# Diagonal of the row factors in the output ring, four loads of x together, and block sums' transfers on GpSimd

## The chip, the cores and the metric

The kernel runs on one core of one Trainium2 chip. The metric is the device time of one execution in microseconds. The time before is the median of three executions; a profile of one execution stands beside it.

## What is computed

The reference is one encoder layer on two token sequences, x_prompt (1024 tokens) and x_sample (2048 tokens) of 1024 channels, each with 16 learned meta tokens put in front. Cut to what matters:

```python
xn = rmsnorm(h, g_pre)
proj = xn @ w_in + b_in                 # 6672 columns: q, k, v, z of both branches, gates
ya = neighbourhood_attention(q, k, v, rpb) * silu(na_z) @ w_a
yb = mlstm_branch(qk, v, gates, o) * silu(ml_z) @ w_b       # both directions, chunks
y  = (sigmoid(ga) * ya + sigmoid(gb) * yb) @ w_out
out = h + rmsnorm(y, g_post)            # meta tokens dropped
```

All of it is float32. A product is made of three matmuls on a high and a low part of each operand (high x high, high x low, low x high), so every operand is first split: the high part is a ScalarE copy to the rounded type fp32r, the low part a VectorE subtraction.

## The kernel before

The program is written as two generators. `dense` makes the large products: the input projection in groups (`PLAN`: a sequence s, a block t0 of 1024 tokens, and a set of columns), then the output stage. `sparse` makes the mLSTM scan and the attention. `run` interleaves the two by estimated cost, and that fixes the order of TensorE's instructions. The order on the other engines (VectorE, ScalarE, GpSimd, and SP, which issues nearly all transfers) is set when the program is built, by a scheduler that simulates times. Each engine then runs its own queue in order.

**x.** A block of 512 tokens is held transposed in a pair of tiles xh and xl. `build_half` makes the pair beside the last products of the block before. For x_sample it loads four token tiles (`tokens`, SP, L398), sums their squares (`rsum`, ScalarE, L355), takes the reciprocal root on VectorE (`rsqrt8`), and writes the four row factors onto the diagonals of a 128 x 512 tile (`rdiag`, two operations on VectorE at L369 and two on ScalarE at L367). TensorE multiplies this by a matrix of ones (`rrows`, L375), which spreads the factors over all partitions, and ScalarE copies them out (L376). The transposed x comes in four loads of 512 KB (`xtload`, SP, L405); VectorE multiplies each with the factors (L527, two for each load), then each is split (L534 and L535). Token tiles and x loads share one ring, xr, of four tiles. The diagonal is written into the last token tile, so the fourth x load waits until the matmul has read it.

**The ring st.** `fm_evac` takes results of the projection out of PSUM into tiles named st, a ring of four in the pool wp, from which SP stores them (L698, L689). Columns with a SiLU, NZ and MZ, take two of these tiles (L678, L679, L680), the others one. A tile of a ring is given out again in the order of the program: the fifth takes the place of the first, once the first has been read.

**Block sums.** Where two halves of 512 tokens use the same weights, blocks of two by two are multiplied with seven products in place of eight (`sgates`, `_sw_order`). That needs sums of weight blocks and of x blocks. They are made as side work, a step every few products (`beside`):

- `wprep` does it for the gate columns: two loads of raw weights into pr (L579), four pairs of results in the one tile po (ScalarE L592, VectorE in `sub` at L571), eight stores (L596).
- `nprep` does it for the attention columns in the ring xr: two loads (L608), results split by ScalarE (L619) and VectorE (in `op` at L604), eight stores (L623, L624).
- `tprep` does it for x, four steps e for each of two blocks: eight stores a step (L653) into DRAM tensors t0h, t0l to t3h, t3l, which `tload` reads back later.

GpSimd (POOL) has little to do: memsets of a border column of the convolution's input raw (L1394, L1396), of the sums ss (L349) and of the scan's first state st (L1539, a tile of its own pool), some small copies, and the loads of the attention's constants (L1077, L1164).

Of the kernel before, what the change touches and what calls it, by code (L numbers as in the profile page):

```python
# [10 lines left out]
F32 = mybir.dt.float32  # L11
# [7 lines left out]
P = 128  # L19
TCARGS = dict(schedule_with_timeline_sim=True)  # L20
D = 1024
# [14 lines left out]
HALF = 528  # L36
# [17 lines left out]
PAIRS = [tuple(c[2 * p:2 * p + 2]) for c in (N_COLS, FM_COLS[24:]) for p in range(len(c) // 2)]  # L54
# [3 lines left out]
def _weight_units():  # L58

    return ([("i", x, P) for x in FM_COLS] + [("t", *c, a) for c in TM_COLS for a in range(2)]  # L60
            + [("m", f, P) for f in range(KT)] + [("o", c, a) for c in range(4) for a in range(2)])
# [76 lines left out]
class K:  # L138
# [327 lines left out]
    def build_half(self, s, t0, res):  # L466

        nc, wp = self.nc, self.wp
        if (s, t0) in self.xkept:
            assert not self.xput  # L470
            yield
            yield "scaled"
            x = []
            for name, part in zip(("xh", "xl"), self.xkept[s, t0]):
                x.append(wp.tile([P, KT, HALF], F32R, name=name, bufs=2))
                for k in range(0, KT, 4):
                    nc.sync.dma_start(x[-1][:, k:k + 4, :512].bitcast(F32), part[:, k:k + 4, :])
                yield
            res.append(tuple(x))
            return  # L480
        if s == 0:
            xts = self.xnext
            self.xnext = None
            while self.rwait:
                yield "wait"
            self.early = False
            yield "scaled"
            g = self.gpre
            p = self.psum("sm", [P, 512])
            nc.tensor.matmul(p[:, :KT], self.ident, g, start=True, stop=True)  # L490
            g = self.cp.tile([P, KT], F32, name="gx")
            nc.vector.tensor_copy(g, p[:, :KT])
            x, r = self.xparts(), []
            for e in range(4):
                self.xsplit(x, xts[e], e, 0, g)
                self.wflush(2)
                yield
            res.append(tuple(x))
            self.xkeep(s, 0, self.xs[0], NM)
            self.xkeep(s, t0, x)  # L500
            yield from self.rsum(self.toks, r)
            nc.vector.tensor_copy(self.rc[:, 4:8], r[0])
            dg = self.rdiag(r[0], self.toks[0][0])

            def rows():
                self.rrows(dg, self.rr[:, 1], "sm")
                self.RD = self.dp.tile([P, D], F32, name="rrd")
                nc.sync.dma_start(self.RD[:, :], self.rr.rearrange("p a t -> p (a t)"))
                self.xp.close()
                self.wside = self.wprep()  # L510
                self.sides.append([self.wside, 3])
            self.rwait[s, t0] = rows
        else:
            bp = self.bp
            toks, r = self.tokens(s, t0, range(4), bp, 4), []
            yield
            yield from self.rsum(toks, r)
            dg = self.rdiag(r[0], toks[3][0])
            xts = [self.xtload(s, t0, e, bp, 4) for e in range(3)]
            yield  # L520
            rr = bp.tile([P, 512], F32, name="rx", tag="thT", bufs=1)
            self.rrows(dg, rr, "pj")
            xts.append(self.xtload(s, t0, 3, bp, 4))
            yield
            for k in range(KT):
                v = xts[k // 2][:, k % 2]
                nc.vector.scalar_tensor_tensor(v, v, self.gpre[:, k:k + 1], rr, op0=ALU.mult, op1=ALU.mult)  # L527
                if k % 2:
                    yield
            yield "scaled"  # L530
            x = self.xparts()
            for e in range(4):
                h = x[0][:, 2 * e:2 * e + 2, :512]
                nc.scalar.activation(h, xts[e], AF.Copy)  # L534
                nc.vector.tensor_tensor(x[1][:, 2 * e:2 * e + 2, :512], xts[e], h.bitcast(F32), op=ALU.subtract)  # L535
                yield
            res.append(tuple(x))
            self.xkeep(s, t0, x)
# [28 lines left out]
    def wprep(self):  # L567

        nc = self.nc
        unit = {k: j for j, k in enumerate(_weight_units())}  # L570
        sub = lambda o, a, b: nc.vector.tensor_tensor(o, a, b, op=ALU.subtract)  # L571
        self.pq = ExitStack()
        pool = self.pq.enter_context(self.tc.tile_pool(name="pq", bufs=1, side="right", reuse_waits="tile"))
        for p in range(6, 14):
            if p == 12:
                self.sides[0][1] = 6
            raw = pool.tile([P, 2, 2, 512], F32, name="pr", bufs=1)
            for f in range(2):
                nc.sync.dma_start(raw[:, f].rearrange("p a c -> p (a c)"), self.i["wu"][unit["i", PAIRS[p][f], P], :, :D])  # L579
            for _ in range(3):  # L580
                yield
            for f, ops in ((0, ("11", "12")), (1, ("21", "22")), (1, ("s3", "s1")), (0, ("s2", "s4"))):
                if ops[0] == "s3":
                    nc.vector.tensor_tensor(raw[:, 1, 1], raw[:, 1, 0], raw[:, 1, 1], op=ALU.add)
                    sub(raw[:, 1, 0], raw[:, 0, 0], raw[:, 1, 0])
                    yield
                if ops[0] == "s2":
                    sub(raw[:, 0, 0], raw[:, 1, 1], raw[:, 0, 0])
                    sub(raw[:, 0, 1], raw[:, 0, 1], raw[:, 0, 0])
                    yield  # L590
                o = pool.tile([P, 2, 2, 512], F32R, name="po", bufs=1)
                nc.scalar.activation(o[:, :, 0], raw[:, f], AF.Copy)  # L592
                sub(o[:, :, 1], raw[:, f], o[:, :, 0].bitcast(F32))
                for q, op in enumerate(ops):
                    d = self.qd[p, op] = self.dp.tile([P, D], F32, name=f"q{p}{op}")
                    nc.sync.dma_start(d[:, :], o[:, q].rearrange("p a c -> p (a c)").bitcast(F32))  # L596
                yield
                yield

    def nprep(self):  # L600

        nc = self.nc
        unit = {k: j for j, k in enumerate(_weight_units())}
        op = lambda o, a, b, x=ALU.subtract: nc.vector.tensor_tensor(o, a, b, op=x)  # L604
        for p in range(6):
            r0, r1 = [self.bp.tile([P, 2, 512], F32, name="xr", bufs=4) for _ in range(2)]
            for f, r in enumerate((r0, r1)):
                nc.sync.dma_start(r.rearrange("p a c -> p (a c)"), self.i["wu"][unit["i", PAIRS[p][f], P], :, :D])  # L608
            for _ in range(2):
                yield  # L610
            op(r1[:, 1], r1[:, 0], r1[:, 1], ALU.add)
            op(r1[:, 0], r0[:, 0], r1[:, 0])
            yield
            op(r0[:, 0], r1[:, 1], r0[:, 0])
            op(r0[:, 1], r0[:, 1], r0[:, 0])
            yield
            for r, ops in ((r1, ("s3", "s1")), (r0, ("s2", "s4"))):
                hi = self.bp.tile([P, 2, 512], F32, name="xr", bufs=4)
                nc.scalar.activation(hi.bitcast(F32R), r, AF.Copy)  # L619
                op(r.bitcast(F32R), r, hi)  # L620
                for q, o in enumerate(ops):
                    d = self.qd[p, o] = self.dp.tile([P, D], F32, name=f"q{p}{o}")
                    nc.sync.dma_start(d[:, :512], hi[:, q])  # L623
                    nc.sync.dma_start(d[:, 512:], r[:, q])  # L624
                yield

    def tprep(self, s, t0):

        nc, dp = self.nc, self.dp
        self.TD[s, t0] = [[dp.tile([P, 4, 512], F32, name=f"t{j}{part}{t0}") for part in "hl"] for j in range(4)]  # L630
        td = self.TD[s, t0]
        while len(self.xs) < 2:
            yield
        (h0, l0), (h1, l1) = self.xs
        for e in range(4):
            ks = slice(2 * e, 2 * e + 2)
            r0, r1, ta, hi = [self.bp.tile([P, 2, 512], F32, name="xr", bufs=4) for _ in range(4)]
# [10 lines left out]
            for a, b, js in todo:  # L648
                nc.scalar.activation(a.bitcast(F32R), b, AF.Copy)
                nc.vector.tensor_tensor(b.bitcast(F32R), b, a, op=ALU.subtract)  # L650
                for q, j in enumerate(js):
                    for d, x in zip(td[j], (a, b)):
                        nc.sync.dma_start(d[:, e, :], x[:, q] if len(js) > 1 else x)  # L653
                yield


# [1479 lines left out]
```

## Time and profile before

| what | value |
|---|---|
| time, median of 3 | 2702.35 us (2702.05 to 2705.8) |
| profiled execution | 2705.33 us; its span, first to last instruction, 2703.3 us |
| mean granted TensorE clock | 0.995 |
| busy: TensorE, weight loads | 2658.4 us (98%), 2345.6 us (87%) |
| busy: VectorE, ScalarE, GpSimd | 1910.4 us (71%), 1418.5 us (52%), 17.4 us (1%) |
| transfers | 783.72 MB, mean 290 GB/s |

The profile's engines are PE (matmul) and PEld (weight load) for TensorE, DVE for VectorE, ACT for ScalarE, POOL for GpSimd, and SPq for SP's queue. A name such as L369 is a line of the kernel; work in a helper has the helper's line. In a row of the timeline the bracket holds the engine's idle time before the instruction and what ended it. The share of the granted clock is of full speed.

### The profile page before, as it was taken

How to read it: one execution, taken by the hardware profiler on the slowest of the kernel's cores; microseconds unless marked ns; L12 is line 12 of the kernel's file. 1: busy time of each engine (PE TensorE's matmuls, PEld its weight loads, DVE VectorE, ACT ScalarE, POOL GpSimd, SP SyncE). 2: the span in 40 equal slices, each digit the busy share in tenths (PEclk: the TensorE clock that was granted, in tenths of full speed). 3: DMA queues.
4: the chain of work that ended last, by engine and by line, in shares of the span. 5: the costliest groups of instructions: out<-in, count | busy, mean ns of one | idle time of the engine just before them, and what ended most of it. 6: DMA issues, size and time to landing. Idle time of an engine off the chain costs nothing.

```text
span 2703.3 us, 47407 instructions
## 1 busy us (share of the span) xinstructions
PE 2658.4 (98%) x16000; PEld 2345.6 (87%) x16000; DVE 1910.4 (71%) x5234; ACT 1418.5 (52%) x3350; POOL 17.4 (1%) x100
## 2 busy tenths in 40 slices
PE   9999998999999999999999999999999999999998
PEld 7898897789987999878888888888889888989888
DVE  5444687978648888446866767658478989897954
ACT  6322555565345654356655566555355655656521
POOL 0000000000000000000000000000000000000000
PEclk9999998999999999999999999999999999999999
DMA  9988887899986898798889988895769798998965
GB/s 373 344 323 316 306 302 277 295 348 345 317 270 228 295 349 298 248 305 259 262 288 329 368 288 258 282 344 189 219 221 303 250 312 257 309 294 262 333 230 202
DMA packets 405986, 783.72 MB, mean 290 GB/s; under 512 B 51472, under 2 KB 180448, under 8 KB 404208
## 3 DMA queue, kind: packets, MB, share of 16 engines
q1 hardware_dynamic: 404624, 778.01, 85.6%
q0 software_dynamic: 1120, 2.69, 0.4%
q8 instruction: 127, 2.08, 0.3%
q14 instruction: 115, 0.94, 0.1%
HBM read 531.66 MB, written 248.88 MB: 289 GB/s over the span
## 4 chain that ended last, share of the span: by engine, by line
PE 70%; DVE 6%; DMA 5%; ACT 2%; issue 1%; SPq 0%; DVEq 0%; ACTq 0%
PE pj L202 8%; PE pj L203 8%; PE pj L204 8%; PE pj L955 6%; PE pj L957 6%; PE pj L956 6%; PE pj L1898 3%; PE pj L1899 3%; PE pj L1900 3%; PE pj L762 3%; PE pj L763 3%; PE pj L764 3%; PE sm L1247 2%; PE tr L1232 2%; DMA stk<-nq 1%
## 5 line engine op out<-in xcount | busy, mean ns | idle before, releaser
L202 PE MATMUL pj<-xh,whi 128*128 128x512 f32 (+1 forms) x992 | 385.5, 389 | 2.7 <-ACT st L679 1.5
L203 PE MATMUL pj<-xl,whi 128*128 128x512 f32 (+1 forms) x992 | 375.3, 378 | 0.1
L204 PE MATMUL pj<-xh,wlo 128*128 128x512 f32 (+1 forms) x992 | 374.7, 378 | 0.2 <-DVE wlo L304 0.2
L762 PE MATMUL pj<-whi,xh 128*128 128x256 f32 (+1 forms) x1152 | 329.7, 286 | 0.0
L763 PE MATMUL pj<-wlo,xh 128*128 128x256 f32 (+1 forms) x1152 | 325.0, 282 | 0.6 <-DMA wlo<-wl 0.6
L764 PE MATMUL pj<-whi,xl 128*128 128x256 f32 (+1 forms) x1152 | 324.7, 282 | 0.0
L204 PEld LDWEIGHTS pj<-xh,wlo 128*128 128x128 f32 x992 | 188.0, 189 | 37.3 <-DVE wlo L304 0.4
L1898 PE MATMUL pj<-whi,mh 128*128 128x256 f32 x768 | 219.6, 286 | 0.7 <-DMA whi<-wh 0.7
L763 PEld LDWEIGHTS pj<-wlo,xh 128*128 128x128 f32 x1152 | 217.0, 188 | 1.0 <-DMA wlo<-wl 0.8
L202 PEld LDWEIGHTS pj<-xh,whi 128*128 128x128 f32 x992 | 188.2, 190 | 33.8 <-ACT st L679 2.0
L762 PEld LDWEIGHTS pj<-whi,xh 128*128 128x128 f32 x1152 | 217.1, 188 | 0.2
L764 PEld LDWEIGHTS pj<-whi,xl 128*128 128x128 f32 x1152 | 217.0, 188 | 0.0
L1900 PE MATMUL pj<-whi,mlo 128*128 128x256 f32 x768 | 216.4, 282 | 0.0
L1899 PE MATMUL pj<-wlo,mh 128*128 128x256 f32 x768 | 216.3, 282 | 0.0
L203 PEld LDWEIGHTS pj<-xl,whi 128*128 128x128 f32 x992 | 188.4, 190 | 28.9 <-issue 1.0
L202 PE MATMUL pj<-yh,whi 128*128 128x512 f32 x384 | 154.1, 401 | 0.0
L203 PE MATMUL pj<-yl,whi 128*128 128x512 f32 x384 | 150.8, 393 | 0.8 <-DVE yl L1800 0.8
L204 PE MATMUL pj<-yh,wlo 128*128 128x512 f32 x384 | 151.2, 394 | 0.0
L1898 PEld LDWEIGHTS pj<-whi,mh 128*128 128x128 f32 x768 | 145.2, 189 | 1.8 <-DMA whi<-wh 0.9
L1899 PEld LDWEIGHTS pj<-wlo,mh 128*128 128x128 f32 x768 | 145.4, 189 | 0.9
L1900 PEld LDWEIGHTS pj<-whi,mlo 128*128 128x128 f32 x768 | 145.3, 189 | 0.0
L1239 DVE TENSOR_TENSOR pts<-tr,pts 96x384 fp32r<-96x384 f32 (+2 forms) x192 | 118.7, 618 | 32.8 <-ACT pts L1234 31.1
(368 smaller groups left out, 6739.2 us busy)
## 6 DMA issues: line engine op xcount, KB each, us to landing
whi<-wh SPq DMA_DIRECT2D x136, 512.0 KB
wlo<-wl SPq DMA_DIRECT2D x136, 512.0 KB
whi<-q SPq DMA_DIRECT2D x63, 512.0 KB
wlo<-q SPq DMA_DIRECT2D x55, 512.0 KB
wraw<-wu SPq DMA_DIRECT2D x48, 512.0 KB
gt<-st SPq DMA_DIRECT2D x96, 256.0 KB
tg<-gt SPq DMA_DIRECT2D x96, 256.0 KB
wh<-whi SPq DMA_DIRECT2D x36, 512.0 KB
```

The lines of the kernel that those rows point to most:

```text
L202: mm(out, ah, bh, start=start, stop=False)
L203: mm(out, ah, bl, start=False, stop=False)
L204: mm(out, al, bh, start=False, stop=stop)
L762: nc.tensor.matmul(o, xh, wh, start=k == 0, stop=False)
L763: nc.tensor.matmul(o, xh, wl, start=False, stop=False)
L764: nc.tensor.matmul(o, xl, wh, start=False, stop=k == KT - 1)
L955: mm(bank, w[:, 0, k], xh[:, k], start=fresh and k == 0, stop=False, skip_group_check=True)
L956: mm(bank, w[:, 0, k], xl[:, k], start=False, stop=False, skip_group_check=True)
L957: mm(bank, w[:, 1, k], xh[:, k], start=False, stop=k == 3, skip_group_check=True)
L1898: nc.tensor.matmul(o, mh[:, k, xs], wh, start=clear > 0 and k == 0, stop=False)
L1899: nc.tensor.matmul(o, mh[:, k, xs], wl, start=False, stop=False)
L1900: nc.tensor.matmul(o, ml[:, k, xs], wh, start=False, stop=clear < 2 and k == KT - 1)
```

## The change

There are three parts.

- The diagonal of the row factors is written into a tile of the ring st and no more into the last token tile. All four x loads are then issued in one step; the fourth was issued a step later, after the matmul.
- The loads and stores of `wprep`, `nprep` and `tprep` are issued by GpSimd in place of SP.
- In `tprep` the x sums 0 and 1 lie in one DRAM tensor for the high parts and one for the low parts, and one transfer of 512 KB stores both sums of a part; before it was one transfer of 256 KB for each. `self.TD` hands out slices of them, so the loads that read them back are as before.

```diff
-            dg = self.rdiag(r[0], toks[3][0])
-            xts = [self.xtload(s, t0, e, bp, 4) for e in range(3)]
+            dg = self.rdiag(r[0], wp.tile([P, HALF], F32, name="st", bufs=4))
+            xts = [self.xtload(s, t0, e, bp, 4) for e in range(4)]
             yield
             rr = bp.tile([P, 512], F32, name="rx", tag="thT", bufs=1)
             self.rrows(dg, rr, "pj")
-            xts.append(self.xtload(s, t0, 3, bp, 4))
             yield
...
             for f in range(2):
-                nc.sync.dma_start(raw[:, f].rearrange("p a c -> p (a c)"), self.i["wu"][unit["i", PAIRS[p][f], P], :, :D])
+                nc.gpsimd.dma_start(raw[:, f].rearrange("p a c -> p (a c)"), self.i["wu"][unit["i", PAIRS[p][f], P], :, :D])
...
-                    nc.sync.dma_start(d[:, :], o[:, q].rearrange("p a c -> p (a c)").bitcast(F32))
+                    nc.gpsimd.dma_start(d[:, :], o[:, q].rearrange("p a c -> p (a c)").bitcast(F32))
...
             for f, r in enumerate((r0, r1)):
-                nc.sync.dma_start(r.rearrange("p a c -> p (a c)"), self.i["wu"][unit["i", PAIRS[p][f], P], :, :D])
+                nc.gpsimd.dma_start(r.rearrange("p a c -> p (a c)"), self.i["wu"][unit["i", PAIRS[p][f], P], :, :D])
...
-                    nc.sync.dma_start(d[:, :512], hi[:, q])
-                    nc.sync.dma_start(d[:, 512:], r[:, q])
+                    nc.gpsimd.dma_start(d[:, :512], hi[:, q])
+                    nc.gpsimd.dma_start(d[:, 512:], r[:, q])
...
-        self.TD[s, t0] = [[dp.tile([P, 4, 512], F32, name=f"t{j}{part}{t0}") for part in "hl"] for j in range(4)]
-        td = self.TD[s, t0]
+        t01 = [dp.tile([P, 2, 4, 512], F32, name=f"t01{part}{t0}") for part in "hl"]
+        td = {j: [dp.tile([P, 4, 512], F32, name=f"t{j}{part}{t0}") for part in "hl"] for j in (2, 3)}
+        self.TD[s, t0] = [[t[:, 0] for t in t01], [t[:, 1] for t in t01], td[2], td[3]]
...
-                for q, j in enumerate(js):
-                    for d, x in zip(td[j], (a, b)):
-                        nc.sync.dma_start(d[:, e, :], x[:, q] if len(js) > 1 else x)
+                for q, x in enumerate((a, b)):
+                    nc.gpsimd.dma_start(t01[q][:, :, e, :] if len(js) > 1 else td[js[0]][q][:, e, :], x)
```

## The prediction

> **What bounds the kernel now.** I read the page first, then the stretches of 60 us, then TensorE's timeline at the places where it stood still, and from there the queues that it waited for.
>
> ```profile
> PE 2658.4 (98%) x16000; PEld 2345.6 (87%) x16000; DVE 1910.4 (71%) x5234; ACT 1418.5 (52%) x3350; POOL 17.4 (1%) x100
> ...
> q1 hardware_dynamic: 404624, 778.01, 85.6%
> q0 software_dynamic: 1120, 2.69, 0.4%
> ...
> PE 70%; DVE 6%; DMA 5%; ACT 2%; issue 1%; SPq 0%; DVEq 0%; ACTq 0%
> ```
>
> TensorE is busy for 2658.4 of 2703.3 us, so all its idle time is 44.9 us, and its order is fixed by the program. The change takes no matmul away. It can win only idle time, and the time in which the clock is halved. GpSimd is nearly empty and its queue of transfers carries 0.4%.
>
> ```profile
> 420.00:480.00 60.00, 51.75 (x217) 41.64 (x216) 46.05 (x108) 36.85 (x82) 0.51 (x4) 0.89 0.80 286
> 480.00:540.00 60.00, 55.60 (x262) 45.79 (x262) 54.09 (x159) 34.78 (x83) 0.10 (x1) 0.94 0.81 286
> 540.00:600.00 60.00, 59.38 (x328) 50.84 (x327) 46.70 (x113) 38.17 (x93) 0.41 (x3) 1.00 1.00 353
> ...
> 780.00:840.00 60.00, 56.88 (x281) 46.30 (x280) 44.48 (x109) 37.61 (x76) 0.00 (x0) 1.00 0.65 219
> ```
>
> The columns are the stretch, its length, and busy time of PE, PEld, DVE, ACT, POOL, then granted clock, DMA share and GB/s. Two stretches stand out: 420 to 540 us loses 12.7 us of TensorE and runs below full clock. That is where the first two halves of x_sample are built. 780 to 840 loses 3.1. Inside the first there are three gaps:
>
> ```profile
> 432.12 0.47 PE L202 MATMUL sm<-vwh,kth 16*128 16x130 f32 x1 [3.00 <-ACT kth L1522]
> ...
> 460.09 0.55 PE L1648 MATMUL sc<-q,kh 128*128 128x256 f32 x1 [4.31 <-DVE nwy L166]
> ...
> 509.06 0.45 PE L202 MATMUL sm<-v,sh 128*128 128x130 f32 x1 [4.40 <-DVE num L1688]
> ...
> 2225.37 0.41 PE L1200 MATMUL sm<-kd,stk 128*128 128x384 f32 x1 [2.12 <-DVE yg L1262]
> ```
> ```profile
> 432.00:439.00 7.00, 6.88 (x18) 5.46 (x19) 6.70 (x12) 1.77 (x5) 0.00 (x0) 0.52 0.50 165
> 460.10:466.50 6.40, 6.40 (x22) 5.64 (x23) 4.97 (x16) 3.34 (x10) 0.20 (x2) 0.53 1.04 413
> 509.00:516.00 7.00, 6.94 (x23) 5.80 (x24) 6.86 (x34) 2.47 (x7) 0.10 (x1) 0.65 0.39 115
> 2225.00:2232.00 7.00, 6.26 (x49) 6.09 (x50) 6.16 (x15) 6.88 (x17) 0.00 (x0) 1.00 0.89 248
> ```
>
> I call the first three A, B and C. They cost 3.00 + 4.31 + 4.40 = 11.7 us of standstill. After each the clock is about halved: 7.0 x 0.48 = 3.4, 6.4 x 0.47 = 3.0 and 7.0 x 0.35 = 2.5 us, together 8.8. The gap of 2.12 left the clock at 1.00. So a gap that falls from 3 us to about 2 gives back its clock loss too, and all three together are worth 20.5 us. Nothing else in the kernel comes near that. The Trainium skill (TensorE: Matmul & The Clock Gate, Part 1) puts the drop at an idle window of about 3.4 us; here a gap of 3.00 was enough, and the measurement decides. By the page's figure A would have cost no clock time and the sum below would lose 3.4 us of its gain.
>
> **Part 1: the moved transfers on SP.** The loops of wprep (8 x 10), nprep (6 x 10) and tprep (2 x 4 x 8) issue 204 transfers on SP. Afterwards 80 + 60 + 2 x 4 x 6 = 188 are issued by GpSimd; bytes are the same.
>
> ```profile
> 401.98 0.84 SPq L596 DMA_DIRECT2D q11s<-po  x2
> ...
> 407.90 0.97 SPq L579 DMA_DIRECT2D pr<-wu  x2
> ...
> 422.03 0.42 SPq L1456 DMA_DIRECT2D va<-mv  x1
> ...
> 424.66 0.38 SPq L698 DMA_DIRECT2D nz<-st  x1
> ```
> ```profile
> 427.19 0.42 ACT L1628 ACTIVATE v<-va 128x260 fp32r<-128x260 f32 x1 [3.92 <-DMA va<-mv]
> ...
> 431.82 0.25 ACT L1522 ACTIVATE kth<-tr 16x128 fp32r<-16x128 f32 x1
> ```
>
> These rows are the cause of A: ScalarE stood 3.92 us for va, did its backlog, and only then made kth. In the 20 us before 422.03 SP issued nearly without a pause, and of that 0.84 + 0.97 = 1.81 us were moved transfers. I take these 1.81 us as the time by which va can be issued earlier. The bounds are 0, if va's issue waited for its buffer and not for the queue, and 3.0, all of A.
>
> The Trainium skill (DMA: Bandwidth & Descriptors, Issuing engines are not separate DMA queues) says that issuing from several engines saves only the issue time, since the transfers share the same engines. That speaks against expecting more than this 1.81 us, and by that rule the 1.00 DMA share of 540 to 600 would stay.
>
> ```profile
> L1164 POOL DMA_DIRECT2D kx<-masks x10: 512/512/542, 729.3 to 2412.4; - x10
> ...
> DMA to landing us min/median/max: 3.9/6.1/9.7
> ```
> ```profile
> L596 SPq DMA_DIRECT2D q<-po x32: 319/426/1147, 78.8 to 614.9; - x32
> ...
>   DMA q<-po: 9.1, 4
> ```
>
> The columns are min/median/max in ns. On GpSimd an issue takes 0.51 us where SP takes 0.43: 188 x 0.51 = 96 us on an engine with 17.4 us of other work, so I take the issues themselves as free. What is new is a wait: GpSimd's stores wait for VectorE's po (L571) or xr, and its loads for a free pr or xr slot. Behind them stand GpSimd's memsets of raw, ss and st, for which the convolution on ScalarE (L1406), the row sums and VectorE wait. The other cost is the landing: ScalarE waited 9.1 us in 4 waits for the stores of the one po buffer, and GpSimd's smaller transfers (128 to 256 KB) land after 6.1 us in the median. Bounds: below nothing, since the stores leave SP's line of waiting transfers; and above by one new gap of A's kind, 3.0 + 3.4 = 6.4 us, for each place where the slack is gone. I take 0, by the 96 us.
>
> **Part 2: x's four loads together.**
>
> ```profile
> 68.85 0.33 SPq L405 DMA_DIRECT2D xt<-xt  x1
> ...
> 70.61 1.01 SPq L405 DMA_DIRECT2D xt<-xt  x2
> ...
> 431.96 0.35 SPq L405 DMA_DIRECT2D xt<-xt  x1
> ...
> 489.34 0.42 SPq L405 DMA_DIRECT2D xt<-xt  x1
> ```
> ```profile
> 487.32 4.07 DVE L527 SCALAR_TENSOR_TENSOR xt<-xt,gpre,rx 128x512 f32<-128x512 f32 x6
> ...
> 499.37 1.41 DVE L527 SCALAR_TENSOR_TENSOR xt<-xt,gpre,rx 128x512 f32<-128x512 f32 x2
> ...
> 506.72 1.22 DVE L535 TENSOR_TENSOR xl<-xt,xh 128x1024 fp32r<-128x1024 f32 x1
> ...
> 508.64 0.47 DVE L1688 TENSOR_TENSOR num<-sm,num 128x128 f32<-128x128 f32 x2
> ```
>
> Now the fourth load waits until TensorE has read the diagonal out of its buffer, at 431.96 and 489.34; afterwards it waits only for the row sums. In the second build VectorE does six products at 487.32, and the last two 8 us later, with their split at 506.72, directly ahead of the L1688 for which TensorE stands in C. If the 1.41 + 1.22 = 2.63 us move ahead, C falls to 1.77 and keeps its clock. Bounds: 0, because VectorE has no idle time between the rows and the total ahead of L1688 need not shrink, and 4.40 + 2.5. I take 2.63 + 2.5 = 5.1, since the work would then run with the first six products, ahead of the scan's steps.
>
> **Part 3: the diagonal in the ring st of four.**
>
> ```profile
> 65.98 0.51 DVE L369 TENSOR_SCALAR xr<-ident,nwy 128x128 f32<-128x128 f32 x2
> ...
> 426.70 1.02 PE L375 MATMUL pj<-xr,ones 128*128 128x512 f32 x2
> ```
> ```profile
> L367 ACT ACTIVATE xr<-ident,nwy x10: 386/388/404, 46.2 to 791.7; 128x128 f32<-128x128 f32 x10
> ...
> 635.28 3.74 DMA szg<-sz
> ```
>
> For the first build the diagonal was written at 66 us and read at 426.70. In the ring its slot is that of the fourth allocation before it. The step falls after two NZ columns, which take two tiles each, so the slot is that of the first of them, stored by the nz issue at 424.66. With the 3.74 us that another load of 256 KB took, it comes free at 428.4. The four operations then cost ScalarE 2 x 0.39 = 0.78 us and VectorE 0.51, in the stretch of A, where before they cost nothing. In the other builds the ring holds one-tile columns or older ones, and the slot is free before the matmul. I charge 0.78 us to A; bounds 0 and the rival below.
>
> **Sum.** A: 3.00 - 1.81 + 0.78 = 1.97, under the 2.12 that kept the clock: gain 1.03 + 3.36 = 4.4 us. C: 5.1 us. B: nothing. Together 9.5 us. The profiled execution took 2705.33 us (span 2703.3 and 2.0 around it), 3.0 more than the median of 2702.35; a difference of 9.5 against that median gives 2693.
>
> **The rivals.** *No change that counts: 2702.* VectorE's work in 470 to 512 is the limit of C, and va's issue waits for its buffer. For it: no idle time on VectorE ahead of L1688. Against it: SP's crowded 20 us.
>
> *Slower by the ring: 2708.* TensorE's L375 at 426.70 waits for the slot. At 3.74 us landing it stands until 428.4 + 0.78 = 429.2; with a landing of 6 us until 431.4, and ScalarE and VectorE, in order, stand in front of the same slot. Then kth comes about 4 us later, and the delay reaches B by another 2: +6. It decides from a landing of about 5 us. For it: the 3.92 us that va needed in the same stretch. Against it: ScalarE was idle until 427.19 anyway.
>
> *Slower by GpSimd's queue: 2715.* In the full stretch (DMA share 1.00) or in 420 to 540, the stores of po land later or a memset stands behind a waiting store, ScalarE waits, and two new gaps of 6.4 us appear: +12.8. It decides where the slack of po's reuse, now overrun in 4 waits of 9.1 us, is overrun by 2 us more.
>
> ```profile
> L1225 DVE TENSOR_SCALAR prb<-prb,sm 128x288 f32<-128x288 f32 (+3 forms) x57 | 22.6, 396 | 1.0
> L1774 DVE TENSOR_SCALAR hb<-hb,mv,nwy 128x128 f32<-128x128 f32 x32 | 8.9, 343 | 0.1
> ```
>
> If these VectorE operations (31.5 us of the 795 us from 295 to 1090) held up GpSimd's issues, 4% of 96 us would be hit, some 4 us over many places: it adds to this rival's chance, not to the sum. The Trainium skill (SBUF — State Buffer, the "DVE blocks DMA" trap) states such a lock; no row here shows one.
>
> **How the numbers follow.** Forecast 0.43; no change 0.22; ring 0.17; GpSimd's queue 0.18. The likeliest case gives 2693, with 2682 (all three gaps gone, 20.5 us) to 2697 as its own range. The whole range is 2682 to 2716. A measurement of this kernel can tell about 0.2%, 5.4 us, from no change: faster 0.43, same 0.22, slower 0.35.
>
> **What would show it.** Right: TensorE's gap near 432 at or under 2.1 us with clock 1.00 behind it; va issued before 421; L527 as one row of eight in each build; the gap near 509 under 2 us; L596, L608, L623, L624 and L653 on POOL at about 0.5 us each. Wrong: a TensorE wait at L375 for DVE or ACT, with the granted clock halved at 427 (the ring); waits of ACT L592 for q<-po above 20 us in sum, or TensorE gaps between 540 and 1080 where there are next to none now (GpSimd); or A, B and C as they are.

## The result

| kernel | median, us | against the kernel before (95%) |
|---|---|---|
| before, beside these runs | 2703.35 (4 runs) | |
| after the change | 2717.84 (2714.61 to 2721.02, 4 runs) | 1.0052 (1.0035 to 1.0070) |
| after the change, run again later | 2716.26 (6 runs) | 1.0049 (1.0032 to 1.0067) |

The change makes the kernel about 0.5% slower, 14 us, where 9.5 us of gain were forecast. The profiled execution of the changed kernel took 2721.02 us with a span of 2719.2. From about L520 on its line numbers are one lower than before: L1627 here is L1628 there.

The first rows are the page of the changed kernel, as quoted of the kernel before:

```profile
PE 2666.7 (98%) x16000; PEld 2350.2 (86%) x16000; DVE 1911.2 (70%) x5234; ACT 1416.9 (52%) x3350; POOL 119.9 (4%) x288
...
q1 hardware_dynamic: 375248, 700.41, 77.7%
q0 software_dynamic: 23072, 80.29, 8.0%
```

The move was made: GpSimd went from 17.4 to 119.9 us, and its queue carries 80.29 MB where it had 2.69 (the columns are packets, MB, share). TensorE's busy time grew by 8.3 us with the same 16,000 matmuls in the same order. Nearly all of that is half-clock time, not work: the records of the clock hold 27.7 us at half speed before and 43.1 us after, and half of the difference is 7.7 us. TensorE's timeline shows the places:

```profile
319.28 0.69 PE L1518 MATMUL tr<-ident,kf 128*128 128x128 f32 x2 [6.09 <-DVE kf L1482]
435.79 1.22 PE L375 MATMUL pj<-st,ones 128*128 128x512 f32 x1 [2.75 <-ACT st L367]
464.89 0.55 PE L1647 MATMUL sc<-q,kh 128*128 128x256 f32 x1 [4.40 <-DVE nwy L166]
495.97 0.35 PE L1647 MATMUL sc<-q,kh 128*128 128x256 f32 x1 [2.25 <-DVE den L1696]
514.89 0.30 PE L202 MATMUL sm<-v,sh 128*128 128x130 f32 x1 [1.90 <-DVE num L1687]
554.12 0.36 PE L202 MATMUL sm<-vwh,kth 128*128 128x260 f32 x1 [1.49 <-DVE st L1549]
1070.45 0.78 PE L1246 MATMUL sm<-pts,vt 104*128 104x256 f32 x2 [1.94 <-ACT prb L1214]
1561.19 0.50 PE L954 MATMUL pj<-xh,whi 128*128 128x512 f32 x1 [1.76 <-ACT pj L990]
```

A's gap at L202 for kth is gone, and one of nearly the same size stands at L375; B is as it was; C is 1.90, but with a new gap of 2.25 ahead of it. The gap of 6.09 at 319 was 1.47 before. As the matmuls are the same and in the same order, the delay of each can be subtracted between the two traces: the changed kernel loses 6.3 us in 300 to 320 us, wins 3.7 in 420 to 520, loses 6.0 in 540 to 580, 3.7 in 1060 to 1080 and 3.6 in 1540 to 1560; smaller steps make up the rest, and 15.9 us stand at the end. Each trace is one execution: the merge of the token sums alone, which costs nothing, ends 4.0 us ahead of the kernel before when its trace is read in this way, so single steps of 1 to 2 us say little. The second profile of the changed kernel loses 6.7 us in 300 to 320 again, but wins nothing in 420 to 520.

The stretches of the same trace right behind some of these gaps (stretch, length, busy times, granted clock, DMA share, GB/s):

```profile
496.00:500.00 4.00, 4.00 (x14) 3.26 (x15) 4.00 (x7) 3.58 (x6) 0.00 (x0) 0.63 0.77 242
515.00:519.00 4.00, 4.00 (x20) 3.35 (x21) 3.97 (x20) 0.95 (x4) 0.00 (x0) 1.00 0.81 226
...
1070.50:1074.50 4.00, 4.00 (x20) 4.00 (x21) 2.66 (x9) 0.28 (x1) 0.86 (x2) 0.57 1.01 374
1561.20:1565.20 4.00, 4.00 (x11) 3.20 (x12) 0.51 (x1) 0.55 (x1) 0.00 (x0) 0.60 1.05 363
```

Gaps of 2.25, 1.94 and 1.76 us are each followed by a clock near 0.6; the one of 1.90 is not. A gap under 2 us is no safe gap; the last section shows what tells them apart.

### The profile page after: what moved, and what is told of

Same layout as the page of the kernel before. It is cut to its first block, busy times and chain, and to the rows that moved or that the text cites. A ratio compares the mean times of both kernels' runs of the same rounds, so it can differ in the third digit from the quotient of the medians.

```text
span 2719.2 us, 47465 instructions
## 1 busy us (share of the span) xinstructions
PE 2666.7 (98%) x16000; PEld 2350.2 (86%) x16000; DVE 1911.2 (70%) x5234; ACT 1416.9 (52%) x3350; POOL 119.9 (4%) x288
## 3 DMA queue, kind: packets, MB, share of 16 engines
q0 software_dynamic: 23072, 80.29, 8.0%
## 4 chain that ended last, share of the span: by engine, by line
PE 48%; DMA 3%; DVE 3%; ACT 1%; issue 0%; SPq 0%; DVEq 0%; ACTq 0%
PE pj L954 6%; PE pj L956 5%; PE pj L955 5%; PE pj L202 5%; PE pj L203 5%; PE pj L204 5%; PE pj L1897 3%; PE pj L1898 3%; PE pj L1899 3%; PE sm L1246 2%; PE tr L1231 1%; DMA whi<-wh 1%; DMA xl<-xl 1%; PE sm L204 1%; PE sm L203 1%
## 5 line engine op out<-in xcount | busy, mean ns | idle before, releaser
L202 PE MATMUL pj<-xh,whi 128*128 128x512 f32 (+1 forms) x992 | 386.5, 390 | 2.8 <-ACT st L678 1.9
L202 PEld LDWEIGHTS pj<-xh,whi 128*128 128x128 f32 x992 | 188.8, 190 | 34.5 <-ACT st L678 2.8
L202 PE MATMUL pj<-yh,whi 128*128 128x512 f32 x384 | 154.1, 401 | 0.0
L1233 ACT ACTIVATE pts<-tr 96x384 fp32r<-96x384 f32 (+2 forms) x192 | 103.6, 539 | 86.5 <-PE tr L1231 85.9
```

Source lines behind the costliest of these rows:

```text
L202: mm(out, ah, bh, start=start, stop=False)
```

## Experiments

Times are medians; the kernel before had 2702.3 to 2704.5 beside each group. Ratios are against it.

### One part at a time

Ring and four loads, all transfers on SP:

```diff
-            dg = self.rdiag(r[0], toks[3][0])
-            xts = [self.xtload(s, t0, e, bp, 4) for e in range(3)]
+            dg = self.rdiag(r[0], wp.tile([P, HALF], F32, name="st", bufs=4))
+            xts = [self.xtload(s, t0, e, bp, 4) for e in range(4)]
```

> The diagonal in the ring st and x's four loads together; all transfers stay on SP as before. Ring theory (the late ring slot makes TensorE wait at L375 and the diagonal no longer made at 66 us shifts ScalarE's order): the whole loss is here, 2712 to 2718 against 2703, with the gap of 2.75 us at L375 near 436, and the gap of 6.09 us at L1518 near 319 too. GpSimd theory (the 188 transfers on the second queue do the harm): 2696 to 2700, since C still falls from 4.40 to about 1.9 and gives 5 us, and no gap of over 2 us near 319 or 554. Order theory (every edit moves the build's order of ScalarE and VectorE by a few places, and the harm comes from such places wherever they fall): gaps at other places than after's, and a sum that the other two do not give.

Measured 2708.40, 1.0013 (1.0003 to 1.0023): in neither range. TensorE waits 4.17 us at L375, and there is no gap of over 1.4 us near 319.

The ring alone, the fourth load apart as before:

> The diagonal in the ring st, the three loads and the fourth apart as before, all transfers on SP. Ring theory: TensorE waits 4 to 9 us at L375 near 430 in place of A's 3.0; 2704 to 2710. Loads theory: C as before at 4.4 or later. If 2708 as with the four loads (2708.4), the loads together did nothing there.

Measured 2708.06, 1.0018 (1.0009 to 1.0027). So the loads together add nothing that can be told from noise, and the kernel with the ring is some 5 us slower. Two of TensorE's waits in its trace:

```profile
428.86 1.90 PE L375 MATMUL pj<-st,ones 128*128 128x512 f32 x2 [3.94 <-ACT st L367]
```
```profile
589.36 0.48 PE L763 MATMUL pj<-wlo,xh 128*128 128x264 f32 x1 [2.69 <-DMA wlo<-wl]
```

The wait at L375 takes the place of A's: over 420 to 440 this trace loses nothing against the kernel before. Its largest step, 3.6 us, is at 580 to 600, behind the second wait. So where the ring's 0.18% sits is not shown. This kernel has a new order of instructions too, and the ring was not measured with the order held and all transfers on SP.

All transfers on GpSimd with the merged sums, the rest as before:

> All transfers of the block sums by GpSimd, two sums by one, the diagonal and x's loads as before. GpSimd theory: slower, 2712 to 2720: A, B and C stay as in the kernel before (11.7 us of standstill) and the new gaps near 319 (6 us) and 554 (2 to 4 us) stand in it, with ScalarE's wait for raw above 5 us near 550. Ring theory: 2700 to 2704, no gap near 319. Order theory: slower or faster by up to 10 us with gaps at places of its own.

Measured 2713.16, 1.0029 (1.0016 to 1.0043): the time of the GpSimd theory, but without its gap near 319; the gap at 555 is there with 2.29 us.

Only the weights' sums (L579, L596) on GpSimd:

> Only the weights' sums (L579 loads, L596 stores) by GpSimd, the rest as before. GpSimd theory: if the weights' transfers do the harm, 2709 to 2716 with the gap near 319 in it, as they run from 78 to 615 us. Ring theory: 2700 to 2704. Order theory: places of its own.

Measured 2710.66, 1.0026 (1.0016 to 1.0035): again the time of the GpSimd theory without the gap near 319.

Only the two later loops on GpSimd, with the merge:

> Only the sums of the later two loops (L608, L623, L624 and the token sums L653, two by one) by GpSimd; the weights' sums stay on SP. GpSimd theory: the loss near 550 (4 to 6 us) is here if the token sums' 2.5 MB on the second queue delay raw; nothing changes before 500 us, so A and the stretch near 319 are as before: 2704 to 2709. Ring theory: 2700 to 2704. Order theory: places of its own.

Measured 2702.16, 0.9994 (0.9982 to 1.0006): nothing.

The merge alone, on SP:

> Two token sums by one transfer, on SP, nothing else changed: 16 issues of 0.43 us fewer, 6.9 us of SP's line in 500 to 600 and 740 to 880. All theories: no change that counts, 2700 to 2705; if 2708 or more, the merge itself or the order that comes with it costs.

Measured 2701.24, 0.9994 (0.9983 to 1.0005): nothing.

Four loads without the ring: the diagonal goes into rx, the tile that takes the factors afterwards.

```diff
-            dg = self.rdiag(r[0], toks[3][0])
-            xts = [self.xtload(s, t0, e, bp, 4) for e in range(3)]
-            yield
             rr = bp.tile([P, 512], F32, name="rx", tag="thT", bufs=1)
+            dg = self.rdiag(r[0], rr)
+            xts = [self.xtload(s, t0, e, bp, 4) for e in range(4)]
+            yield
```

> The diagonal is written into rx, the tile that takes the factors afterwards, so it needs no slot of the ring and no token tile; x's four loads go together; all transfers on SP. Loads theory (part 2 as forecast: the four loads move 2.63 us of VectorE's work ahead of C): C falls from 4.40 to 1.9 or less and keeps its clock, no wait at L375, 2696 to 2700 against 2703.5. Order theory: L527 becomes one row of eight, but C stays at 4 to 6 us as ScalarE's and VectorE's places move; 2702 to 2708.

Measured 2705.53, 1.0008 (0.9999 to 1.0017), so no gain from the loads. VectorE's timeline shows why (three rows picked, then TensorE's):

```profile
484.99 5.39 DVE L526 SCALAR_TENSOR_TENSOR xt<-xt,gpre,rx 128x512 f32<-128x512 f32 x8 [0.57 <-ACT rx L376]
...
505.67 0.68 DVE L641 TENSOR_TENSOR xr<-xr 128x512 f32<-128x512 f32 x1
506.27 0.68 DVE L643 TENSOR_TENSOR xr<-xr 128x512 f32<-128x512 f32 x1
```
```profile
508.47 0.45 PE L202 MATMUL sm<-v,sh 128*128 128x130 f32 x1 [5.32 <-DVE num L1687]
```

The eight products are one row, as forecast. But the steps L641 and L643 of the x sums (L642 and L644 before, at 509.10 and 509.70, behind the awaited L1688) now stand ahead of the awaited operation, at 505.67 and 506.27. C is 5.32, not 1.77.

The same with the two later loops on GpSimd:

> The diagonal in rx, four loads together, and only the later two loops' transfers (L608, L623, L624, L653, two by one) on GpSimd; the weights' sums stay on SP. If the two gains add (0 to 1.5 us of the later loops alone, 0 to 5 us of the loads), 2696 to 2702; by the order theory up to 2708.

Measured 2707.95, 1.0020 (1.0010 to 1.0030): the gains did not add. Each half alone measured at most 1.0008.

### The order of instructions held fixed

Every edit above also changes the order that the build gives to ScalarE and VectorE. In the changed kernel 642 of ScalarE's 3,032 instructions and 1,248 of VectorE's 5,042 stand at another place than before. A moved order need not cost: counted in the traces, the two later loops alone on GpSimd move 235 of ScalarE's and 499 of VectorE's, and that kernel is not slower. To separate the order from the transfers, an order was written into the program as edges that fix a sequence and wait for nothing:

```python
order = [mine[n] for n in ORDER_OF_THE_OTHER_KERNEL[engine]]
for a, b in zip(order, order[1:]):
    tc.add_manual_dep(b, a.name, mybir.DependencyInfo(mybir.DependencyClass.NoSync, mybir.DependencyReason.DATA), reason="pin")
```

The weights' sums on GpSimd, ScalarE, VectorE and SP in the order of before:

> The weights' sums by GpSimd, as in the run that moved them alone (2710.7 against 2703.7), but every instruction of ScalarE and VectorE, and every remaining one of SP, stands in the order of the kernel before (edges that fix an order and wait for nothing). It keeps the second queue and takes away the new order. Queue theory (the second queue's 1 MB of weights share the 16 engines with the small transfers, so yb's store lands late and SP's line stands behind L1584): still 2708 to 2713, with SP's wait at L1584 above 4 us near 405 and A above 5 us. Order theory (the loss comes from the other places of ScalarE's and VectorE's instructions): back at 2701 to 2705, A at 3.0 or less.

Measured 2703.28, 0.9994 (0.9985 to 1.0003). And with SP free:

> The weights' sums by GpSimd, ScalarE and VectorE held in the order of the kernel before, SP's order free. With SP held too it was 2703.3. Order theory for ScalarE and VectorE: the same, 2702 to 2705. If it is SP's own order that matters (va behind more of the stores), 2708 to 2712, as with no order held (2710.7).

Measured 2701.40, 1.0000 (0.9990 to 1.0010). For these transfers nothing of the 7 us is left once ScalarE and VectorE keep their order: the queue costs nothing that these runs can tell.

The opposite, all on SP, in the order of the weights-on-GpSimd kernel:

> The kernel before, all transfers on SP, with ScalarE's and VectorE's instructions in the order that they have where the weights' sums alone are on GpSimd. It keeps the new order and takes away the second queue. Order theory: 2708 to 2713. Queue theory: 2702 to 2705.

Measured 2707.16, 1.0016 (1.0008 to 1.0025): that order costs by itself 0.16 of the 0.26% that it came with.

The kernel before in the order of the changed kernel:

> The kernel before, all transfers on SP, the diagonal in the token tile and three x loads ahead of the fourth, with ScalarE's and VectorE's instructions in the order that they have after the whole change. Order theory: most of the whole change's loss, 2710 to 2718, with the gap near 319 of about 6 us. Queue and ring theories: 2700 to 2706, no gap of over 2 us near 319.

Measured 2728.16, 1.0091 (1.0078 to 1.0104), above both ranges. An order made for other transfer times costs more than the change did. In its trace 7.4 us are lost at 280 to 300, where TensorE stands 3.49 us for kth and the changed kernel loses nothing, and 5.2 us at 300 to 320. The changed kernel in the order of before:

> The whole change, with ScalarE's and VectorE's instructions in the order of the kernel before; the diagonals alone are free, as their slot in the ring comes later. Order theory: the forecast's place, 2693 to 2703, without the gap near 319 and that near 554. Queue theory: 2710 to 2718, the gap near 554 stays, as raw's landing and the bulk of GpSimd's queue are not touched. Ring theory: 2706 to 2709, with TensorE waiting at L375 near 430.

Measured 2715.06, 1.0044 (1.0033 to 1.0056): the time is in the queue theory's range, not in the order theory's, and 2.20 us of waiting stand at 560. But the two kernels differ at 319 as the order theory has it. TensorE's rows, first the kernel before in the changed order, then the changed kernel in the old order:

```profile
325.75 0.47 PE L1519 MATMUL tr<-ident,kf 128*128 128x128 f32 x1 [5.39 <-DVE kf L1483]
```
```profile
319.12 0.28 PE L1518 MATMUL tr<-ident,kf 128*16 128x128 f32 x1 [1.38 <-DVE kf L1482]
...
433.76 1.22 PE L375 MATMUL pj<-st,ones 128*128 128x512 f32 x1 [8.76 <-ACT st L367]
```

The gap at 319 follows the order, not the transfers. ScalarE's rows say how: first the kernel before, then the changed one.

```profile
304.31 0.51 ACT L1406 ACTIVATE cv<-raw,cw 128x256 f32<-128x256 f32 x1
304.72 1.27 ACT L1499 ACTIVATE vwh<-va,g_wT 128x130 fp32r<-128x130 f32 x4
```
```profile
312.12 1.07 ACT L591 ACTIVATE po<-pr 128x1024 fp32r<-128x1024 f32 x1
314.62 1.28 ACT L1498 ACTIVATE vwh<-va,g_wT 128x130 fp32r<-128x130 f32 x4 [1.43 <-DMA va<-mv]
315.81 0.49 ACT L1405 ACTIVATE cv<-raw,cw 128x256 f32<-128x256 f32 x1
```

The convolution that leads to kf stood ahead of vwh; now it stands behind po (1.07 us of side work) and behind vwh, with its wait of 1.43 for va. kf comes at 318.80, and TensorE waits for it.

With the order held, 8.76 us at L375 remain. ScalarE's rows in that kernel:

```profile
429.56 0.42 ACT L1627 ACTIVATE v<-va 128x260 fp32r<-128x260 f32 x1 [8.28 <-DMA va<-mv]
429.98 0.51 ACT L1405 ACTIVATE cv<-raw,cw 128x256 f32<-128x256 f32 x1
430.39 1.26 ACT L1619 ACTIVATE um<-um,g_a 128x128 f32<-128x128 f32 x4
431.56 0.42 ACT L1547 ACTIVATE st<-sm 128x130 f32<-128x130 f32 x2
431.88 0.67 ACT L677 ACTIVATE st<-pj,bfm 128x512 f32<-128x512 f32 x1
432.45 0.68 ACT L678 ACTIVATE st<-pj,bfh 128x512 f32<-128x512 f32 x1
433.02 0.69 ACT L367 ACTIVATE st<-ident,nwy 128x128 f32<-128x128 f32 x2
```

L367 has no bracket: it does not wait for its slot in the ring. It stands in ScalarE's line behind L1627, which waits 8.28 us for va, and behind five groups after that. In every kernel with the ring TensorE waits at L375 for L367: 2.75 us in the changed kernel, 3.94 with the ring alone, 4.17 with ring and loads, 8.76 here. It is the place in the order that does it: the kernel before in the changed order has no ring, and TensorE waits 2.11 us there too. Most of the 8.76 is the wait for va, not the ring: the next kernel has the same transfers and order without the ring, and stands 6.64 us at A.

### All transfers on GpSimd, order held

> All transfers by GpSimd, two sums by one, as in the run of 2713.2, with ScalarE's and VectorE's instructions in the order of the kernel before. Order theory: 2701 to 2706, without the gap near 554. Queue theory: the gap near 554 stays at 1.5 to 2.3 us (it is there in both kernels that have the weights' and the token sums' transfers on GpSimd, and in neither that has one of the two), and the sum is 2706 to 2713.

Measured 2716.40, 1.0046 (1.0033 to 1.0059): with all three loops the old order does not give the time back. TensorE waits 6.64 us at A and 1.66 at 551.

```profile
433.56 0.47 PE L202 MATMUL sm<-vwh,kth 16*128 16x130 f32 x1 [6.64 <-ACT kth L1522]
```

GpSimd's and SP's issues ahead of A, in this kernel:

```profile
398.04 1.05 POOL L596 DMA_DIRECT2D q11s<-po  x2 [10.12 <-DVE hb L1706]
399.09 1.06 POOL L579 DMA_DIRECT2D pr<-wu  x2
```
```profile
400.20 1.31 SPq L1781 DMA_DIRECT2D yb<-szg  x1
...
409.27 0.34 SPq L1584 DMA_DIRECT2D szg<-sz  x1
```

and SP's in the kernel before:

```profile
400.05 0.40 SPq L1781 DMA_DIRECT2D yb<-szg  x1
...
402.92 0.78 SPq L1584 DMA_DIRECT2D szg<-sz  x1
...
407.90 0.97 SPq L579 DMA_DIRECT2D pr<-wu  x2
```

On SP the 1 MB of pr stood eight us behind yb's store. GpSimd issues it right behind 1 MB of po, just ahead of yb; the load szg, which waits for yb's store, goes 9.1 us after it where it was 2.9, and everything behind it in SP's line waits too. So relieving SP did not make its line faster. Which goes first matters: in the six traces in which GpSimd has begun to issue pr ahead of yb's store, szg follows yb after 9.0 to 9.9 us; in the four traces in which yb goes ahead of pr, both of the changed kernel among them, after 4.2 to 6.5. But the weights' kernel with SP held too has the same delay (9.7 us) and is not slower, with the same order of ScalarE and VectorE as here. There TensorE's wait for kth is split into 1.82 and 2.51 us; why the delay costs time in the one and not in the other is not shown.

The same with SP held too:

> All transfers by GpSimd, two sums by one, with ScalarE, VectorE and SP held in the order of the kernel before (2716.4 with SP free). If SP's order was the cause, 2702 to 2706 and A back at 2.5 to 3; if the queue's bulk is, 2711 to 2717 with the gaps near 433 (above 5 us), 551 and 991 still there.

Measured 2708.37, 1.0025 (1.0016 to 1.0033), between the two ranges. The gap at 551 is gone, A is split into gaps of 2.40, 1.29 and 0.93, and the largest new gap is late:

```profile
951.86 0.54 POOL L608 DMA_DIRECT2D xr<-wu  x1
952.39 1.09 POOL L624 DMA_DIRECT2D q0s<-xr  x2
958.65 0.54 POOL L608 DMA_DIRECT2D xr<-wu  x1 [5.17 <-DMA q0s<-xr]
```
```profile
968.21 0.69 DVE L604 TENSOR_TENSOR xr<-xr 128x512 f32<-128x512 f32 x1 [3.56 <-DMA xr<-wu]
```
```profile
978.37 0.62 PE L1247 MATMUL sm<-pts,vt 104*128 104x256 f32 x3 [3.78 <-ACT prb L1215]
```

nprep's second load waits 5.17 us on GpSimd for a slot whose stores are still under way in GpSimd's own queue, VectorE waits 3.56 for the load, ScalarE's L619 for VectorE, and the attention's prb stands behind L619. Before, VectorE waited 0.50 at that place and TensorE 0.72.

Only the stores on GpSimd, all held:

> Only the stores (L596, L623, L624, L653, two sums by one) by GpSimd; the loads of the weights (L579, L608) stay on SP in their places, and ScalarE, VectorE and SP are held in the order of the kernel before. Bulk theory (1 MB of weights and 1 MB of sums enter the second queue as soon as a buffer is free, beside or ahead of the small va, raw and yb): without the loads yb's store lands in under 4 us again (L1584 issued within 4 us of yb, not 9), A stays at 3.0, and the time is 2700 to 2705. If the stores' bulk is enough, 551 keeps its gap and it is 2706 to 2712.

Measured 2710.11, 1.0030 (1.0018 to 1.0041), against the bulk theory's main branch. yb's delay fell to 5.7 us, A is 3.48 and no wait stands at 551, but nearly all the loss is again one gap, of 4.73 us at 977. So the loads are not needed for the loss: the stores are enough. The way there is another, though, as nprep's load is on SP: ScalarE stands first for the load stk, 3.95 us where it stood 0.25 before. From there to 977 the chain was not followed.

```profile
963.61 0.63 ACT L1167 ACTIVATE qB<-stk 64x512 fp32r<-64x512 f32 x1 [3.95 <-DMA stk<-nq]
```
```profile
977.24 0.41 PE L1247 MATMUL sm<-pts,vt 104*128 104x256 f32 x1 [4.73 <-ACT prb L1215]
```

### Do the parts add up?

The whole change with the diagonal in rx:

> The whole change, but the diagonal in rx in place of the ring's tile. If the parts add up (ring 0.18%, GpSimd 0.29%, the loads together up to 0.08%), the loss of the ring goes and 2710 to 2714 remains, with no wait at L375 and A back at L202 for kth. If the parts only cost in their own order of instructions, it falls anywhere from 2702 to 2720.

> The whole change once more, beside the kernel above and the kernel before on one chip: 2714 to 2720 (0.4 to 0.7% slower), the sum of the ring's 0.18% and GpSimd's 0.29% being 0.47%.

Measured 2711.36, 1.0036 (1.0022 to 1.0050) without the ring and 1.0049 (1.0032 to 1.0067) for the whole change beside it. The medians add up: ring 0.18% + GpSimd 0.29% = 0.47% for 0.49 to 0.52%, but each has an interval of 0.1 to 0.2% to both sides, so that is weak evidence. The places do not add up. Without the ring 6.02 us stand at 319, and A has shrunk to 0.58. The rows show why. TensorE is 7.3 us late ahead of A and ScalarE's v 6.6. Of the eight um operations (L1620 before) that stood between v and kth two now stand ahead of v and four behind kth, so that ScalarE needs 2.8 us from v to kth where it needed 4.6. So most of A's gain there comes from the new order (1.9 us), and less from an earlier v (0.7).

No kernel here beats the kernel before: the best ratios, 0.9994, include 1.

## Why the prediction was wrong, step by step

**A, 1.81 us from SP's line: the lead came, the gain did not.** The changed kernel's rows:

```profile
427.14 0.37 SPq L1455 DMA_DIRECT2D va<-mv  x1
```
```profile
432.27 0.42 ACT L1627 ACTIVATE v<-va 128x260 fp32r<-128x260 f32 x1 [4.23 <-DMA va<-mv]
```

va is issued 5.1 us later than before. TensorE is 6.3 to 7.4 us late there, so against its work va does come 1.2 to 2.3 us earlier, about as forecast. It gave no shorter wait: ScalarE stands 4.23 us for va (3.92 before), and TensorE now stands at L375. The stretch 420 to 440 wins 2.7 us in one profile of the changed kernel and 1.1 in the other, where 4.4 were forecast; the trace of the merge alone, whose transfers come after 500 us, differs there by 1.7. Nor did SP issue nearly without a pause ahead of va: issues fill 15.2 of those 20 us, and in the rest SP stood. Where the weights' sums alone were moved, va was issued at 425.66 against 422.03, as SP's line stood behind L1584, and A was 5.81. The Trainium skill's rule (DMA: Bandwidth & Descriptors, Issuing engines are not separate DMA queues), that other issuers save issue time alone as the transfers share the engines, fits the delay of yb: 9.1 us behind the loads of pr on GpSimd's queue, 2.9 in the kernel before.

**The ring, 0.78 us: mis-sized, and the rival had the wrong reason.** The kernel with the ring alone is 0.18% slower, about 5 us, and where that time goes is not shown. What the rows show is the wait at L375. The work is small (0.69 us of ScalarE), and it does not wait for its slot; it is late because it stands behind a waiting instruction on an in-order engine. Before, the four operations were done at 66 us. The forecast looked at what a step costs and at its slot, not at who stands in front of it. The rival's sign (TensorE at L375) and its size (2708) were right; a late slot, its reason, is in no row.

**C, 5.1 us: right in place, wrong in use.** The products did move together (one row of eight with the diagonal in rx, four and four with 0.4 us between them in the changed kernel, below). The lower bound that the prediction kept, 0 because VectorE has no idle time there, is what happened: other VectorE work filled the place. The 1.90 of the changed kernel is not this gain; with the 2.25 just ahead of it it makes 4.15, against 4.40. Over 480 to 520 one profile wins 0.7 us and the other loses 2.4, where 5.1 were forecast.

```profile
492.69 2.73 DVE L526 SCALAR_TENSOR_TENSOR xt<-xt,gpre,rx 128x512 f32<-128x512 f32 x4
495.82 2.73 DVE L526 SCALAR_TENSOR_TENSOR xt<-xt,gpre,rx 128x512 f32<-128x512 f32 x4
```

**GpSimd, 0: mis-sized.** All its transfers together cost 0.29%, some 8 us. The rival at 2715 (12.8 us more) was nearer in size, but its mechanism did not come. ScalarE's waits for the stores of po did not grow above 20 us; they fell from 14.0 us (9.1 and 4.9) to 2.0 (1.6 and 0.4). What came was the changed order, and with the order held yb's late store and nprep's load behind its own stores; in the changed kernel itself szg follows yb after 4.2 us. The issues themselves are nearly as cheap as the 0.51 us taken: medians of 0.53 to 0.56 us, 0.68 for the merged ones, the longest 0.82. No row shows them held by VectorE, so for the lock that the Trainium skill states (SBUF — State Buffer, the "DVE blocks DMA" trap) nothing speaks here.

**The clock.** The sum rested on one gap of 2.12 us that kept its clock. 1.76, 1.94 and 2.25 lost it. The last section works out why: what counts is the idle time within a piece of 3.41 us, and that gap was split over two. The Trainium skill (TensorE: Matmul & The Clock Gate, Part 1) puts the drop at an idle window of about 3.4 us; the length agrees, but here half of it idle was enough. Idle time rose by 7.6 us and TensorE's busy time by 8.3, so about half of the loss in this trace is clock.

**What was left out: the order.** The forecast moved single steps and kept all others in place. But the build sets the order of ScalarE and VectorE by simulated times, so an edit of transfers reshuffles both. At 319 us that alone made a gap of 5.39 us in place of 1.47 (6.09 in the changed kernel), shown from both sides. With the order held nothing is left of the cost of the weights' sums. But the order is not the whole cost of the change: with it held, all transfers on GpSimd still cost 0.25 to 0.46%, and the stores alone 0.30%.

**Left open.** Whether the ring's 0.18% is the ring's or its order's was not tested. TensorE's wait at L954 (1.76 us at 1561) has no cause here; the second profile of the changed kernel does not have it. The losses near 551, 1070 and 1170 were not taken apart; the one at 551 goes when SP's order is held. For all transfers with everything held, the price at 978 is shown, and only argued to be the queue's: with the stores alone the loss has the same place, but begins at another load.

## What to carry to other kernels

Ask of a moved step not only what it costs and what it waits for, but who stands in front of it on its in-order engine, and what goes earlier once it is out of a line: a line that was full also held the bulk back. If the build sets the order from simulated times, an edit of one thing moves others; hold the order fixed to see what the edit itself does, before you explain a difference of half a per cent. And a gap that shrinks need not have shrunk by the term that was forecast: A's fall to 0.58 came mostly from a moved order.

## What the runs showed of the hardware

A halved clock followed a gap of 1.76 us, while 1.90 and 2.12 us kept full speed. In each of the twenty traces here, all stretches of half clock begin a whole number of times 3.41 us apart. Cut into pieces of 3.41 us on that grid (the first 10 and the last 12 us left out), TensorE went from full to half clock only behind a piece with at least 1.43 us of idle time in sum, and always behind one with more than 1.87; in between it went either way. The gaps of 1.94 and 1.76 us each lie in one piece. The one of 1.90 is split into 1.14 and 0.76, the one of 2.12 into 0.67 and 1.45, and one of 2.67 us, at 1104.62 in the kernel before with the changed order, lies over two pieces with 1.57 and 1.11 us and kept full speed too. So whether a gap of 1.5 to 3 us costs clock depends on where it falls.

On GpSimd's queue the landing grew with what was in front. In the kernel with all transfers there and the old order of ScalarE and VectorE, the profile's issues between 536 and 550 us (form, count, KB each, median us to landing) read:

```profile
q12s<-po POOLq DMA_DIRECT2D x2, 512.0 KB, 8.4
pr<-wu POOLq DMA_DIRECT2D x2, 512.0 KB, 11.7
...
t2h<-xr POOLq DMA_DIRECT2D x1, 256.0 KB, 6.8
t2l<-xr POOLq DMA_DIRECT2D x1, 256.0 KB, 13.0
```

Two stores of the same 256 KB took 6.8 and 13.0 us, the later one behind some 2 MB of other transfers on its queue. SP moves 2.71 MB beside GpSimd's 2.87 in these 14 us, so what the queue and what the shared engines add is not separated. The prediction had taken 6.1, from ten loads on a nearly empty queue.
